# Heads 72 to 79 of a tree attention kernel stored by GpSimd in seventeen small DMAs instead of by GpSimd and SyncE in three

## The chip, the cores and the metric

The kernel runs on one core of a Trainium2 chip. The core has five instruction streams: TensorE (PE in the profile), VectorE (DVE), ScalarE (ACT), GpSimd (POOL) and SyncE (SP). Bytes between the device memory and the on-chip memory are moved by 16 DMA engines; DMAs are issued here from GpSimd (queue q0 of the profile), SyncE (q1) and ScalarE (q10). The metric is the device time in microseconds (us); lower is better.

## The reference

Q, K and V are float32 tensors of 8 batches, 12 heads, 512 positions and 64 dimensions. The positions are the nodes of a binary heap, and each node attends to itself and its ancestors:

```python
mask[i, i] = 1
parent = i
while parent > 0:
    parent = (parent - 1) // 2
    mask[i, parent] = 1

scores = np.einsum('bhqd,bhkd->bhqk', Q, K) * scale
scores = scores + (1 - mask) * (-1e9)
weights = np.exp(scores - np.max(scores, axis=-1, keepdims=True))
weights = weights / (np.sum(weights, axis=-1, keepdims=True) + 1e-10)
return np.einsum('bhqk,bhkd->bhqd', weights, V).astype(np.float32)
```

The output is as large as one input: 96 heads (batch and head together) of 128 KB each, 12.6 MB.

## The kernel before, in words

The 96 heads are worked through in 48 steps of two heads. A step makes the scores of its pair (`scores1`, `scores2`, with the mask put in by small matmuls of codes), takes exponentials on ScalarE, multiplies by V on TensorE (`values`, L551) and divides by the row sums on VectorE (`norm`, a reciprocal at L581 and a product at L583). Transposes of K and Q for later steps and copies of V rows (`spread`, L336) go between.

`norm` writes into a buffer `of` of eight heads (128 partitions, each with 8 heads x 4 positions x 64 numbers). There are twelve such groups and eleven buffers. A partition holds four neighbouring positions of a head, which are 1 KB in a row of the output. `store` (L590) writes some heads and some partitions of such a group to the output; every store has the line L591.

The order of work on each engine is written out by hand. GpSimd has one list of its own, made by `pool_program` (L606): loads of K, Q and V, which change float32 to bf16 on the way, copies of V rows, and stores of whole groups. `ready` (L648) says from which step on the next entry may be emitted, and entries are emitted in the list's order, so a GpSimd instruction that waits holds up everything behind it in the list. The last entries are stores: groups of eight heads up to head 71, then heads 72 to 75, then heads 80 to 87.

SyncE has the rest: at step 41 (`APART_AT`) `store_apart` (L601) stores heads 76 to 79 in two DMAs, of 60 and of 68 partitions, and the last four steps' heads (88 to 95) go out in three stores of two heads and one of one head, with the very last head on ScalarE (L768 to L771).

Waits between engines and on DMAs are put in by the framework when the program is compiled. A DMA that GpSimd issues gets one of eight semaphores in turn. In the compiled program each carries a wait for its semaphore's previous use, and so for the landing of the DMA eight places before it, beside any wait for data.

Of the kernel before, what the change touches and what calls it, by code (L numbers as in the profile page):

```python
# [119 lines left out]
def kernel(  # L120
# [7 lines left out]
    nc = tc.nc  # L128
    B, H, S, D = Q.shape
    P = nc.NUM_PARTITIONS  # L130
# [6 lines left out]
    KB, VB = 8, 16  # L137
# [307 lines left out]
    def turn(name, i):  # L445
        heads = [head(i + b, a) for b in range(2 if i >= WIDE else 1) for a in range(2)]
        assert all((name, h) in issued for h in heads), (name, i)
        {"kst": (narrow_k, wide_k), "qst": (narrow_q, wide_q)}[name][i >= WIDE](i)
        return i + (2 if i >= WIDE else 1)
# [4 lines left out]
    def scores1(i):  # L454

        sp = psS.tile([P, 2, 512], fp32, name="s1")
        for a in range(2):
            nc.tensor.matmul(  # L458
                out=sp[:, a, :],
                lhsT=(k1code if i < WIDE else k1wide)[64 * a:64 * a + CODE_ROWS, :],  # L460
                rhs=(q1code[64 * a:64 * a + CODE_ROWS, :] if i < WIDE
                     else q1wide[64 * a:64 * a + CODE_ROWS, :, :]),
                start=True, stop=False,
            )
        for a in range(2):
            nc.tensor.matmul(  # L466
                out=sp[:, a, :], lhsT=keys(i, a, TOP),
                rhs=qTs[i][64 * a:64 * a + 64, :, :].rearrange("p t c -> p (t c)"),
                start=False, stop=True,
            )  # L470
        et = etpool.tile([P, 2, 4, 128], bf16, name="e1")
        nc.scalar.activation(  # L472
            out=et[:, :, :, :].rearrange("p a t c -> p (a t c)"),
            in_=sp[:, :, :].rearrange("p a c -> p (a c)"),
            func=AF.Exp, scale=scale,
        ) if i < WIDE else nc.scalar.activation(  # L476
            out=et[:, :, :, :].rearrange("p a t (r u) -> p a (t r) u", u=2),
            in_=sp[:, :, :].rearrange("p a (u c) -> p a c u", u=2),
            func=AF.Exp, scale=scale,
        )  # L480
        ets[i] = et
# [92 lines left out]
    def norm(i):  # L574
        j, r = divmod(i, 4)
        if r == 0:
            ofs[j] = opool.tile([P, 8, 4, D], fp32, name="of")
        o4 = obs[i][:, :, 0:260].rearrange("p a (t c) -> p a t c", c=D + 1)
        rec = small.tile([P, 2, 4, 1], fp32, name="rec")
        for a, n in ((0, 2),) if i < NP - 1 else ((0, 1), (1, 1)):  # L580
            nc.vector.reciprocal(out=rec[:, a:a + n, :, :], in_=o4[:, a:a + n, :, D:D + 1])  # L581
            h0, h1 = [head(i, x) % 8 for x in (a, a + n - 1)]
            nc.vector.tensor_tensor(  # L583
                out=ofs[j][:, h0:h1 + 1:head(i, 1) - head(i, 0), :, :],
                in0=o4[:, a:a + n, :, 0:D],
                in1=rec[:, a:a + n, :, :].to_broadcast([P, n, 4, D]),
                op=ALU.mult,
            )

    def store(eng, h0, n, step=1, p0=0, p1=P):  # L590
        return eng.dma_start(  # L591
            out=Or[p0:p1, h0:h0 + step * (n - 1) + 1:step, :],
            in_=ofs[h0 // 8][p0:p1, h0 % 8:h0 % 8 + step * (n - 1) + 1:step, :, :].rearrange(
                "p h t d -> p h (t d)"
            ),
        )

    APART, APART_AT, APART_ROWS = 76, 41, 60

    def store_apart():  # L601

        for p0, p1 in ((0, APART_ROWS), (APART_ROWS, P)):
            store(nc.sync, APART, 4, 1, p0, p1)

    def pool_program():  # L606

        ops = [
            (load_k, 2, 2), (load_q, 2, 2), (load_v, 0, 4), (load_v, 4, 4),
            (load_k, 4, 2), (load_k, 6, 2), (load_q, 4, 2), (load_k, 8, 4),  # L610
            (load_q, 6, 2), (load_q, 8, 4), (load_v, 8, 8), (load_k, 12, 4),
            (load_q, 12, 4), (load_k, 16, 4), (load_rows, 1, "upper"),
            (load_q, 16, 4), (load_rows, 1, "even"), (load_k, 20, 4), (load_rows, 1, "odd"),
            (load_q, 20, 4), (load_k, 24, 8), (load_q, 24, 4), (load_rows, 2, "upper"),
            (load_q, 28, 4), (load_k, 32, 4), (load_rows, 2, "even", "odd"),
            (load_q, 32, 8), (load_k, 36, 4), (load_rows, 3, "upper"),
            (spread_pool, (1, "Z0", 8, 16), (1, "Z1", 8, 16), (1, 6, 8, 16), (1, 9, 8, 16)),
            (load_k, 40, 8), (load_q, 40, 8), (load_rows, 3, "even", "odd"), (spread_top, 2),
            (spread_pool, (2, "Z0", 0, 16), (2, "Z1", 0, 16), (2, "X", 0, 16)),
            (spread_top, 3, 0, 4), (load_q, 48, 4),  # L620
            (spread_top, 3, 4, 8), (load_k, 48, 8), (load_q, 52, 4), (spread_top, 3, 8, 12),
            (load_rows, 4, "upper"), (spread_top, 3, 12, 16),
        ]
        loaded, stored = 72, 0
        for h in range(56, NH, KB):
            top = [(spread_top, h // VB + 0)] if h % VB == 8 and 4 <= h // VB + 0 < NH // VB else []
            if top:
                top.append((spread_pool, (h // VB, "Z0", 0, 16), (h // VB, "Z1", 0, 16)))
            ops += [(load_k, h, KB)] + top + [(load_q, h, KB)]
            if h == 64:  # L630
                ops.append((spread_pool, (3, "Z0", 0, 16), (3, "Z1", 0, 16), (3, "X", 0, 16)))
            while loaded < min(h + 32, NH):
                names = ("even", "odd") if loaded % VB else ("upper",)
                ops.append((load_rows, loaded // VB) + names)
                loaded += KB
            if top:
                o = h // VB
                ops.append((spread_pool, (o, "X", 0, 16)))
            if stored + KB + BEHIND <= h + KB:
                ops.append((store, nc.gpsimd, stored, KB))  # L640
                stored += KB
        while stored < NH - KB:
            n = 4 if stored + 4 == APART else KB
            ops.append((store, nc.gpsimd, stored, n))
            stored += KB
        return ops

    def ready(op, i):  # L648

        f, args = op[0], op[1:]  # L650
        if f in (load_k, load_q):
            return 2 * (i + 3) >= args[0] + args[1] - 4 * KB
        if f is load_v:
            return True
        if f is load_rows:
            return 2 * i >= VB * (args[0] - 2)
        if f is spread_pool:
            return 2 * i >= VB * (args[0][0] + 1 - NV) and all(
                part != "X" or ("vt", "M", VB * o + h) in issued
                for o, part, h0, h1 in args for h in range(h0, h1)  # L660
            )
        if f is spread_top:
            return 2 * i >= VB * (args[0] + 1 - NV)
        return 2 * i >= args[1] + args[2]

    BY_VECTOR = {
# [69 lines left out]
    for i in range(NP + 1):  # L736
        steps = FIRST[i] if i < len(FIRST) else "SVK" if i % 2 else "SVQ"
        for step in steps:
            if step == "S" and i < NP:
                scores1(i)  # L740
                scores2(i)
            if step == "V" and i >= 1:
                values(i - 1)
                norm(i - 1)
                valued = True
            if step == "K" and kdone < NP:
                kdone = turn("kst", kdone)
            if step == "Q" and qdone < NP:
                qdone = turn("qst", qdone)
            if step == "W":  # L750
                nc.scalar.copy(
                    out=codes[64:64 + CODE_ROWS, 1280:1536], in_=codes[0:CODE_ROWS, 1280:1536]
                )
            if step == "X":
                spin("s1" if valued else "ob", 2)
            if step == "D":
                spread_by(nc.vector.tensor_copy, BY_VECTOR, STEADY_VECTOR, i)
            if step == "A":
                spread_by(nc.scalar.copy, BY_SCALAR, {}, i)
        if "D" not in steps:  # L760
            spread_by(nc.vector.tensor_copy, BY_VECTOR, STEADY_VECTOR, i)
        if "A" not in steps:
            spread_by(nc.scalar.copy, BY_SCALAR, {}, i)
        pool(i)
        if i == APART_AT:
            store_apart()
        if i >= NP - 3 and i < NP:
            store(nc.sync, head(i - 1, 0), 2, 2)  # L768
    assert not program
# [32 lines left out]
```

## Time and profile before

| | |
|---|---|
| time, median of 2 runs | 134.98 us (134.3 and 135.66) |
| the profiled execution's own time | 134.74 us |
| its span | 132.9 us |
| PE, DVE, ACT, POOL busy | 85%, 76%, 70%, 57% of the span |
| read from and written to device memory | 37.94 MB and 12.58 MB, 380 GB/s over the span |
| last exponential, last product of `norm` | before 125 us, at 126.3 us |
| stores issued by GpSimd | 11, the last at 119.1 us |
| stores issued by SyncE and ScalarE | 6 and 1, from 108.8 to 126.3 us |

The span is the time from the first to the last instruction in the trace; the device time has a little around it. Times in the trace count from the start of the span. In the page's line of 40 slices each digit is the busy share of a slice in tenths. In a timeline row come the start, the duration, the engine, the line, the operation, what it writes and reads, how many, and in brackets how long its engine was idle before it and what ended that. The landing of a DMA is the moment from which whoever waits for it may go on.

### The profile page before, as it was taken

How to read it: one execution, taken by the hardware profiler on the slowest of the kernel's cores; microseconds unless marked ns; L12 is line 12 of the kernel's file. 1: busy time of each engine (PE TensorE's matmuls, PEld its weight loads, DVE VectorE, ACT ScalarE, POOL GpSimd, SP SyncE). 2: the span in 40 equal slices, each digit the busy share in tenths (PEclk: the TensorE clock that was granted, in tenths of full speed). 3: DMA queues.
4: the chain of work that ended last, by engine and by line, in shares of the span. 5: the costliest groups of instructions: out<-in, count | busy, mean ns of one | idle time of the engine just before them, and what ended most of it. 6: DMA issues, size and time to landing. Idle time of an engine off the chain costs nothing.

```text
span 132.9 us, 5533 instructions
## 1 busy us (share of the span) xinstructions
PE 113.1 (85%) x2417; PEld 78.5 (59%) x2417; DVE 100.6 (76%) x249; ACT 93.6 (70%) x151; POOL 76.2 (57%) x112
## 2 busy tenths in 40 slices
PE   6785979999899899989989999996899998989600
PEld 2342765766566577656767575674576775665400
DVE  3439779887999989969797797887779986865600
ACT  4359678988587597858859687686598986869400
POOL 6989635265296979999596796569585400011000
PEclk9999999999999999999999999999999999999965
DMA  3999999999999999999999999999999999999981
GB/s 101 240 188 195 201 196 201 200 202 206 200 202 203 202 204 205 200 206 201 205 204 200 311 256 202 288 280 243 328 219 335 227 299 401 402 400 398 386 321 56
DMA packets 32221, 32.26 MB, mean 243 GB/s; under 512 B 1181, under 2 KB 29469, under 8 KB 32197
## 3 DMA queue, kind: packets, MB, share of 16 engines
q0 software_dynamic: 29824, 29.63, 114.2%
q1 hardware_dynamic: 1813, 1.83, 4.0%
q10 hardware_dynamic: 560, 0.46, 1.2%
q8 instruction: 19, 0.31, 0.9%
q14 instruction: 5, 0.04, 0.1%
HBM read 37.94 MB, written 12.58 MB: 380 GB/s over the span
## 4 chain that ended last, share of the span: by engine, by line
PE 41%; DMA 28%; DVE 11%; POOL 10%; issue 4%; ACT 1%; DVEq 0%; ACTq 0%; POOLq 0%
DMA vst<-in_V_dram 16%; PE ob L551 14%; DMA qst<-in_Q_dram 12%; PE s L458 7%; PE qtp L433 4%; PE ktp L401 4%; PE s L466 4%; PE s L501 4%; PE s L491 4%; POOL vt L336 3%; DVE vt L336 3%; DVE of L583 3%; POOL kst L239 2%; POOL qst L239 2%; POOL vst L239 1%
## 5 line engine op out<-in xcount | busy, mean ns | idle before, releaser
L476 ACT ACTIVATE e<-s 128x1024 bf16<-128x1024 f32 x40 | 41.0, 1024 | 22.0 <-PE s L466 22.0
L551 PE MATMUL ob<-vt,e 128*128 128x65 bf16 (+1 forms) x940 | 37.6, 197 | 3.3 <-DVE of L583 1.4
L551 PEld LDWEIGHTS <-e 128*128 128x128 bf16 (+1 forms) x960 | 30.4, 102 | 11.6 <-DVE of L583 1.5
L507 ACT ACTIVATE e<-s 128x384 bf16<-128x384 f32 x80 | 34.7, 490 | 0.0
L583 DVE TENSOR_TENSOR of<-ob,rec 128x512 f32<-128x512 f32 x47 | 32.5, 691 | 1.6
L336 POOL COPY vt<-vst 32x128 int32<-32x128 int32 (+3 forms) x44 | 27.4, 622 | 6.2 <-DVE vt L336 3.9
L336 DVE COPY vt<-vst 64x1024 bf16<-64x1024 bf16 (+6 forms) x42 | 18.4, 438 | 3.4 <-DMA vst<-in_V_dram 2.8
L458 PE MATMUL s<-codes 40*128 40x512 bf16 x96 | 19.5, 394 | 1.0 <-issue 0.4
L581 DVE RECIPROCAL rec<-ob 128x8 f32<-128x8 f32 x47 | 9.7, 205 | 13.4 <-PE ob L551 12.5
L591 POOL DMA_DIRECT2D out_dram<-of x11 | 9.8, 893 | 17.2 <-DVE of L583 12.7
L466 PE MATMUL s<-kq 64*128 64x512 bf16 x96 | 18.5, 377 | 0.0
L280 POOL DMA_DIRECT2D vst<-in_V_dram x15 | 11.1, 743 | 9.1 <-DMA vst<-in_V_dram 5.6
L501 PEld LDWEIGHTS <-kq 64*128 64x128 bf16 x320 | 12.4, 94 | 5.1 <-issue 0.5
L501 PE MATMUL s<-kq 64*128 64x160 bf16 (+1 forms) x320 | 14.9, 208 | 0.3 <-issue 0.3
L401 PE MATMUL ktp<-ptile,kst 128*64 128x128 bf16 x320 | 12.6, 220 | 2.1 <-DMA kst<-in_K_dram 1.0
L441 DVE COPY kq<-qtp 128x1024 bf16<-128x1024 bf16 x20 | 13.6, 682 | 0.7 <-PE qtp L433 0.7
L433 PE MATMUL qtp<-ptile,qst 128*64 128x128 bf16 x320 | 12.6, 220 | 1.8 <-issue 0.9
L491 PE MATMUL s<-codes 40*128 40x384 bf16 x80 | 13.8, 334 | 0.1
L251 POOL DMA_DIRECT2D qst<-in_Q_dram x13 | 9.5, 728 | 4.7 <-DMA qst<-in_Q_dram 1.7
L251 POOL DMA_DIRECT2D kst<-in_K_dram x12 | 9.2, 763 | 5.0 <-PE s L466 1.5
L401 PEld LDWEIGHTS <-kst 128*64 128x64 bf16 x320 | 9.9, 110 | 2.7 <-issue 1.3
L472 ACT ACTIVATE e<-s 128x1024 bf16<-128x1024 f32 x8 | 8.2, 1023 | 4.6 <-PE s L466 4.5
(42 smaller groups left out, 115.3 us busy)
## 6 DMA issues: line engine op xcount, KB each, us to landing
out_dram<-of POOLq DMA_DIRECT2D x10, 1024.0 KB, 17.3
kst<-in_K_dram POOLq DMA_DIRECT2D x8, 512.0 KB, 15.0
qst<-in_Q_dram POOLq DMA_DIRECT2D x7, 512.0 KB, 15.4
vst<-in_V_dram POOLq DMA_DIRECT2D x12, 256.0 KB, 12.7
vst<-in_V_dram POOLq DMA_DIRECT2D x6, 512.0 KB, 12.8
qst<-in_Q_dram POOLq DMA_DIRECT2D x8, 256.0 KB, 11.0
kst<-in_K_dram POOLq DMA_DIRECT2D x6, 256.0 KB, 11.7
out_dram<-of SPq DMA_DIRECT2D x3, 256.0 KB, 7.3
```

Of the source, the lines that this page charges most:

```text
L251: return nc.gpsimd.dma_start(out=kept[b][:, h0 % KB:h0 % KB + n, :, :].rearrange("p (g x) t d -> p g (x t d)", x=2), in_=wide[:, h0 // 2:( ...
L336: return copy(out=dst, in_=src)
L401: nc.tensor.transpose(out=columns(kp[64 * a:64 * a + 64, :], mixed, (256, 2), (leaves - mixed, 2), (1, 32)), in_=st[:, 2 * i % KB // 2 + a ...
L433: nc.tensor.transpose(out=halves[64 * a:64 * a + 64, :, c:c + 64], in_=st[:, 2 * i % KB // 2 + a, 4 * u + t, :], identity=ptile[:, 0:128],)
L458: nc.tensor.matmul(out=sp[:, a, :], lhsT=(k1code if i < WIDE else k1wide)[64 * a:64 * a + CODE_ROWS, :], rhs=(q1code[64 * a:64 * a + CODE_ ...
L466: nc.tensor.matmul(out=sp[:, a, :], lhsT=keys(i, a, TOP), rhs=qTs[i][64 * a:64 * a + 64, :, :].rearrange("p t c -> p (t c)"), start=False, ...
L476: ) if i < WIDE else nc.scalar.activation(
L491: nc.tensor.matmul(out=flat[:, a, :, :].rearrange("p u (t c) -> p u t c", t=4)[:, :, :, 16:64], lhsT=k2wide[64 * a:64 * a + CODE_ROWS, :], ...
L501: nc.tensor.matmul(out=flat[:, a, :, lo:hi], lhsT=keys(i, a, WTILE2[t]), rhs=qT[64 * a:64 * a + 64, :, lo:hi], start=False, stop=t == 1, s ...
L507: nc.scalar.activation(out=e2s[i % NE][:, a, :, 32:128].rearrange("p t (r u) -> p t r u", u=2), in_=flat[:, a, :, :].rearrange("p u (t r) ...
L551: nc.tensor.matmul(out=ob[lo:hi, a, 65 * t:65 * t + 65], lhsT=e[:, a, PLACE[t], lo:hi], rhs=vt[vtile[tile_v][0]][:, head(i, a) % VB, vtile ...
L583: nc.vector.tensor_tensor(out=ofs[j][:, h0:h1 + 1:head(i, 1) - head(i, 0), :, :], in0=o4[:, a:a + n, :, 0:D], in1=rec[:, a:a + n, :, :].to ...
```

## The change

GpSimd takes over heads 76 to 79 as well. Heads 72 to 75 become eight DMAs of 17, 17, 17, 17, 17, 17, 17 and 9 partitions, heads 76 to 79 become nine of 7, seven times 17, and 2 partitions. An instruction ahead of the first one sets the turn in which GpSimd's DMAs are dealt to DMA engines back to the first engine. The intent of the number 17 is that a DMA of 17 rows isn't divided among engines. `ready` lets each of the two groups go once its four heads are normalised. The two stores of SyncE go away; all other stores stay.

```diff
-    APART, APART_AT, APART_ROWS = 76, 41, 60
-
-    def store_apart():
-
-        for p0, p1 in ((0, APART_ROWS), (APART_ROWS, P)):
-            store(nc.sync, APART, 4, 1, p0, p1)
+    APART = {72: (17,) * 7 + (9,), 76: (7,) + (17,) * 7 + (2,)}
+
+    def store_apart(h0):
+
+        if h0 == 72:
+            nc.gpsimd.inc_swdge_sem([], [], mode="reset_dge_cursor")
+        p0 = 0
+        for n in APART[h0]:
+            store(nc.gpsimd, h0, 4, 1, p0, p0 + n)
+            p0 += n
+        assert p0 == P
...
         while stored < NH - KB:
-            n = 4 if stored + 4 == APART else KB
-            ops.append((store, nc.gpsimd, stored, n))
+            if stored in APART:
+                ops += [(store_apart, h) for h in APART]
+            else:
+                ops.append((store, nc.gpsimd, stored, KB))
             stored += KB
...
+        if f is store_apart:
+            return 2 * i >= args[0] + 4
...
         pool(i)
-        if i == APART_AT:
-            store_apart()
         if i >= NP - 3 and i < NP:
```

On GpSimd's list the cursor instruction and the 17 stores stand behind the store of heads 64 to 71 and ahead of the store of heads 80 to 87.

## The prediction

> **What bounds the kernel now.** I read the page's slices first, then busy time and DMA by stretches, then the timeline of GpSimd, then the DMA issues of short stretches. The page:
>
> ```profile
> span 132.9 us, 5533 instructions
> ...
> DMA  3999999999999999999999999999999999999981
> GB/s 101 240 188 195 201 196 201 200 202 206 200 202 203 202 204 205 200 206 201 205 204 200 311 256 202 288 280 243 328 219 335 227 299 401 402 400 398 386 321 56
> ...
> q0 software_dynamic: 29824, 29.63, 114.2%
> q1 hardware_dynamic: 1813, 1.83, 4.0%
> ```
>
> The DMA engines are busy from the second slice to the last but one. q0 is GpSimd's queue, q1 is SyncE's. After the last loads the stores move some 400 GB/s. The stretches, in columns PE, PEld, DVE, ACT, POOL, granted clock, DMA share, GB/s:
>
> ```profile
> 109.00:112.00 3.00, 2.34 (x58) 1.58 (x51) 2.02 (x6) 1.82 (x4) 0.00 (x0) 1.00 1.03 398
> 112.00:116.00 4.00, 4.00 (x101) 2.92 (x96) 2.78 (x7) 3.44 (x6) 0.00 (x0) 1.00 1.03 397
> 116.00:120.00 4.00, 3.31 (x80) 2.48 (x77) 2.46 (x7) 2.84 (x5) 0.88 (x1) 1.00 1.03 404
> 120.00:124.00 4.00, 3.83 (x70) 2.36 (x70) 1.77 (x4) 3.82 (x8) 0.01 (x1) 1.00 1.02 395
> 124.00:126.00 2.00, 1.06 (x21) 0.74 (x20) 1.73 (x6) 0.49 (x2) 0.00 (x0) 1.00 0.99 382
> 126.00:128.00 2.00, 0.00 (x0) 0.00 (x0) 0.29 (x1) 0.00 (x0) 0.00 (x0) 0.84 0.99 367
> 128.00:130.00 2.00, 0.00 (x0) 0.00 (x0) 0.00 (x0) 0.00 (x0) 0.00 (x0) 0.50 0.71 240
> 130.00:133.00 3.00, 0.00 (x0) 0.00 (x0) 0.00 (x0) 0.00 (x0) 0.00 (x0) 0.50 0.12 41
> ```
>
> Compute is over at about 126.3 and the stores then drain, so the end is a matter of stores. At 397 GB/s a store of 1 MB (8 heads) costs 2.64 us on all engines, and one engine moves 397/16 = 24.8 GB/s. The drain is ragged: what is left after 128 is 2 x 0.71 + 3 x 0.12 = 1.8 us of all 16 engines, yet it takes 3.1 us; the unevenness is worth 1.3 us.
>
> Now GpSimd, which issues all stores but the last few (start, duration, idle before and who ended it):
>
> ```profile
> 70.06 0.66 POOL L280 DMA_DIRECT2D vst<-in_V_dram  x1
> 71.14 0.65 POOL L280 DMA_DIRECT2D vst<-in_V_dram  x1 [0.41 <-DMA qst<-in_Q_dram]
> 72.45 0.90 POOL L591 DMA_DIRECT2D out_dram<-of  x1 [0.67 <-DMA vst<-in_V_dram]
> 74.04 0.76 POOL L251 DMA_DIRECT2D kst<-in_K_dram  x1 [0.69 <-PE s L466]
> ...
> 79.59 0.74 POOL L251 DMA_DIRECT2D qst<-in_Q_dram  x1
> ...
> 82.54 0.91 POOL L591 DMA_DIRECT2D out_dram<-of  x1
> 83.44 0.76 POOL L251 DMA_DIRECT2D kst<-in_K_dram  x1
> 85.16 0.74 POOL L251 DMA_DIRECT2D qst<-in_Q_dram  x1 [0.96 <-DMA qst<-in_Q_dram]
> 86.30 0.91 POOL L591 DMA_DIRECT2D out_dram<-of  x1 [0.40 <-DMA vst<-in_V_dram]
> ...
> 97.81 3.56 POOL L591 DMA_DIRECT2D out_dram<-of  x4
> 103.02 0.89 POOL L591 DMA_DIRECT2D out_dram<-of  x1 [1.66 <-DVE kq L412]
> 105.67 0.76 POOL L591 DMA_DIRECT2D out_dram<-of  x1 [1.76 <-DVE vt L336]
> 119.12 0.90 POOL L591 DMA_DIRECT2D out_dram<-of  x1 [12.69 <-DVE of L583]
> ```
>
> The row at 86.30 is the important one. It is a store, which reads `of` and writes the output, and what let it go is the landing of a load of V. No data joins the two. The DMA issued at 70.06 is the eighth before it, and it landed 15.9 us after its issue (row below), at 86.0. GpSimd's DMAs take eight completion semaphores in turn, and each waits until the one eight before it has landed. In this trace the limit costs GpSimd a few tenths of a us at a time, since what it issues is large.
>
> The landings that the sum needs (us from issue to landing, each DMA alone in its stretch of the DMA view; the fourth row is the store at 119.12):
>
> ```profile
> vst<-in_V_dram POOLq DMA_DIRECT2D x1, 256.0 KB, 15.9
> ...
> out_dram<-of POOLq DMA_DIRECT2D x1, 1024.0 KB, 14.9
> ...
> out_dram<-of POOLq DMA_DIRECT2D x1, 1024.0 KB, 21.2
> ...
> out_dram<-of POOLq DMA_DIRECT2D x1, 1024.0 KB, 9.8
> ...
> out_dram<-of ACTq DMA_DIRECT2D x1, 128.0 KB, 5.3
> ```
>
> The store at 97.81 landed at 112.7, the one at 103.02 (heads 64 to 71) at 124.2, the one at 119.12 (heads 80 to 87) at 128.9, and ScalarE's, issued at 126.3, at 131.6, the last of all. The span ends 1.3 later at 132.9.
>
> **The change, part by part.** *Removed*: one 512 KB store of heads 72 to 75 on GpSimd, and on SyncE the two stores of heads 76 to 79 (60 and 68 rows). *Added on GpSimd*: the cursor instruction and 17 small stores (eight for 72 to 75, nine for 76 to 79), all ahead of the store of heads 80 to 87. Loads and compute keep their place: GpSimd's last load is issued at 94.0, before any of this, and behind the small stores only that one store is queued. Bytes are the same.
>
> *The cursor instruction* has no row. It stands in idle time (1.76 us before the row at 105.67), so between 0 and that it costs nothing; that it waits for the queue to empty is a rival.
>
> *Eight semaphores.* In the compiled program each of the 17, and the store of heads 80 to 87, waits for its semaphore. Numbering the small ones 1 to 17 and the last store 18: numbers 2 and 3 wait for loads, 4 to 8 for the five 1 MB stores issued from 97.81 to 103.02, number 9 for number 1, 10 for 2, 17 for 9, and **18 for number 10**. Today the last store waits at 119.12 for VectorE alone.
>
> Step 1, number 8's gate: heads 64 to 71 must have landed on all engines, 124.2 today. The first of the five landed at 112.7, so without SyncE's stores between them it is 112.7 + 4 x 2.64 = 123.3. Check: from 112 on, SyncE's queue moved 0.24 + 0.09 + 0.10 MB,
>
> ```profile
> q1 hardware_dynamic: 240, 0.24, 16.9%
> ...
> q1 hardware_dynamic: 98, 0.09, 6.8%
> ...
> q1 hardware_dynamic: 102, 0.10, 7.3%
> ```
>
> (stretches 112 to 116, 116 to 120, 120 to 124), 1.1 us at 397 GB/s, which gives 124.2 - 1.1 = 123.1. Bounds: 122.0 (no unevenness, 123.3 - 1.3) and 124.2.
>
> Step 2, number 1 lands. Its 17 rows of 4 KB go to one engine: 69,632 bytes at 24.8 GB/s are 2.8 us, behind that engine's share of the five stores. If the engine runs ahead of the slowest by 2.8 us it adds nothing, if it is the slowest it adds 2.8. No row tells which engine is slow, so I take the middle: 123.3 + 1.4 = 124.7 (bounds 122.0 and 127.0). Number 2 is then as far on the next engine.
>
> Step 3, number 9 goes at 124.7 and number 10 one issue later. An issue of 512 rows took 0.66 us (70.06), one of 1024 rows 0.89; the line through them gives 0.46 for 17 x 4 rows. I take 0.5 (bounds 0.36, the shortest of SyncE's below, and 0.66): 125.2.
>
> ```profile
> L591 SPq DMA_DIRECT2D out_dram<-of x6: 357/390/793, 108.8 to 125.8; - x6
> ...
> kst<-in_K_dram POOLq DMA_DIRECT2D x1, 128.0 KB, 4.5
> ...
> ptile<-tree_eye ACTq DMA_DIRECT2D x1, 64.0 KB, 2.6
> ```
>
> Step 4, number 10 lands. Now its queue is dry, so the start and finish of a DMA, hidden so far by what was queued, show. GpSimd's first load (4.5 us to landing for 128 KB, 0.3 us of transfer) gives 4.2 at most. It shared the engines with 256 + 256 + 120 + 64 KB of other first loads, 1.8 us, which leaves 2.4; the 64 KB load of ScalarE on idle engines also gives 2.6 - 0.2 = 2.4. I take 2.5, with bounds 2.4 and 4.2. Number 10 lands at 125.2 + 2.5 + 2.8 = 130.5. The nine issues from number 9 on would let 18 go at 124.7 + 4.5 = 129.2, so the landing decides: **the last store goes at 130.5 instead of 119.1**.
>
> Step 5, it lands: 130.5 + 2.5 + 2.64 = 135.6. Number 16, issued at 128.2, holds its engine until 133.5 by the same terms, 0.5 longer than the last store would leave it waiting: 136.1. SyncE's and ScalarE's last stores are issued by 126.3 and meet half-empty engines; they land before that.
>
> The Trainium skill, page "DMA: Bandwidth & Descriptors", section on the anatomy of a GpSimd DMA, fits a DMA at 2.0 us plus its bytes at 436 GB/s; by it the last store would take 4.4 us where I have 5.1, and the time would be 0.7 lower. Row and rule can't be told apart on this trace, where GpSimd's later DMAs are always queued.
>
> Sum: landing 136.1, end of span 1.3 later at 137.4, and the profiled execution's own time lies 134.74 - 132.9 = 1.84 above its span: **139.2 us**. The profiled execution of before is 0.24 under the median of the two runs (134.98), so I leave it at 139.2, 3.1% slower.
>
> **The rivals.** *Spread after all (13%).* The small stores go to several engines, two rows each. Number 1 then adds 2 x 4 KB, 0.33 us, instead of 2.8, and number 10 no longer takes 2.8 us. Only issues count: number 8 at 123.3, ten issues of 0.5 to the last store at 128.3, landing 133.4, time 133.4 + 1.3 + 1.84 = 136.6. Against it: 17 rows don't divide; for it: every GpSimd store in this trace was spread. The Trainium skill (same page, section "Why a DMA increments its semaphore by 16 and not by 1") says that the engine count is the largest number up to 16 that divides the rows, so one for 17, but notes an exception on trn2 in which GpSimd's direct copies are spread all the same, by the rows over 16 rounded up. No GpSimd DMA of before has a row count by which the two differ.
>
> *Not slower: the relief decides (6%).* 272 KB of SyncE's stores were drained at a crawl (some 25 packets a us after 116, rows above), ahead of SyncE's last stores. Without them the drain evens out and gains up to 1.3 us: 134.74 - 1.3 = 133.4. It decides only if the last store goes early enough to land by 131.6, so at 131.6 - 5.1 = 126.5 or sooner. That needs numbers 9 to 17 not to hold it, against the row at 86.30.
>
> *One engine for all (3%).* The turn doesn't move on, and all 17 go to the same engine: 1 MB at 24.8 GB/s is 42 us behind 122, the last store's share behind that, some 170 us.
>
> *The cursor waits for the queue (8%).* Number 1 then goes only at 123.3 and lands at 123.3 + 0.5 + 5.3 = 129.1, number 10 at 129.1 + 0.5 + 5.3 = 134.9, the last store at 140.5: 143.7.
>
> **How the numbers follow.** My forecast has 70%. Its own range: all low bounds give 122.0 + 0.36 + 5.2 + 5.0 = 132.6, time 135.7; all high ones 127.0 + 0.66 + 7.0 + 7.3 = 142.0, time 145.1, which needs every term at its worst, so I keep 135.7 to 143.0 for it. With the spread case below (136.6, about 1 us either way) and the waiting cursor at the top, the range is 135.5 to 143.2. About 2% is what a measurement of this kernel can tell from no change, that is up to 137.7 on one side and down to 132.3 on the other. A fifth of my forecast lies under 137.7. Slower: 0.56 of my forecast, 0.03 of the spread case, 0.11 of the last two: 0.70. Faster: a third of the relief, 0.02. Within 2%: 0.28.
>
> **What would show it.** Step 1: numbers 4 to 8 on GpSimd 2.6 us apart, each ended by the landing of a store. Steps 2 to 4: number 9 near 125, the store of heads 80 to 87 near 130, its wait ended by a DMA and no longer by VectorE; landing of a small one after a dry queue near 5.3. Step 5: a DMA share well under 1 from about 124 to 131, with engines idle while stores remain, and then one burst of 1 MB at the end. PE, VectorE and ScalarE unchanged until 126. I am wrong if the last store goes before 127, if the small ones are issued without waits, or if their landings show that engine 0's turn is long past.

## The result, and the profile after

The changed kernel takes 149.44 us (149.06 and 149.81) against 134.98 before: a ratio of 1.1075, with an interval of 1.1007 to 1.1142. (An execution that took over 1.5% longer than the fastest of the same kernel is left out of the times and ratios in this document.) The direction was forecast; the size was not. 139.2 was predicted, in a range that ended at 143.2. So the question for the experiments is what cost 10 us more than the waits that the prediction counted.

The page of the changed kernel, span, slices, packet sizes and GpSimd's queue, and behind it the packet sizes of the kernel before:

```profile
span 146.2 us, 5547 instructions
...
DMA  3999999999999999999999999999999999885371
GB/s 126 211 184 195 198 199 201 201 206 202 201 203 201 204 206 200 204 201 207 199 306 247 202 323 233 314 243 298 260 284 398 402 385 176 119 211 124 57 258 50
DMA packets 35673, 32.31 MB, mean 221 GB/s; under 512 B 5018, under 2 KB 32794, under 8 KB 35650
...
q0 software_dynamic: 33808, 30.21, 108.7%
...
DMA packets 32221, 32.26 MB, mean 243 GB/s; under 512 B 1181, under 2 KB 29469, under 8 KB 32197
```

Up to slice 33 it is the kernel before. In the next two slices the engines still show busy (9 and 8 in the DMA line) while the rate falls from some 400 to 176 and 119 GB/s. The packets tell of what: 5018 are under 512 bytes, where the kernel before has 1181. In the trace 3600 of them are packets of 16 bytes on GpSimd's queue, and the kernel before has none of that size. The stretches of the changed kernel, in the columns of the prediction:

```profile
116.00:120.00 4.00, 3.37 (x78) 2.31 (x72) 2.98 (x8) 2.58 (x6) 1.09 (x2) 1.00 1.01 392
120.00:124.00 4.00, 3.77 (x76) 2.40 (x70) 2.17 (x5) 3.82 (x7) 1.98 (x2) 1.00 1.01 203
124.00:126.00 2.00, 1.23 (x30) 0.86 (x26) 0.18 (x1) 1.45 (x3) 0.75 (x2) 1.00 0.83 72
126.00:128.00 2.00, 0.73 (x17) 0.52 (x14) 1.84 (x6) 0.00 (x0) 1.66 (x3) 0.87 0.93 167
128.00:130.00 2.00, 0.00 (x0) 0.00 (x0) 0.00 (x0) 0.00 (x0) 1.77 (x2) 0.50 0.96 219
130.00:134.00 4.00, 0.00 (x0) 0.00 (x0) 0.00 (x0) 0.00 (x0) 2.32 (x4) 0.50 0.70 166
134.00:138.00 4.00, 0.00 (x0) 0.00 (x0) 0.00 (x0) 0.00 (x0) 3.52 (x4) 0.50 0.35 65
138.00:142.00 4.00, 0.00 (x0) 0.00 (x0) 0.00 (x0) 0.00 (x0) 0.00 (x0) 0.50 0.71 220
```

From 120 to 124 the share is 1.01 at 203 GB/s, half the rate of before, and from 124 to 126 it is 0.83 at 72. That isn't the picture of engines that wait, which the prediction expected. GpSimd's timeline:

```profile
106.16 1.11 POOL L591 DMA_DIRECT2D out_dram<-of  x1 [1.93 <-DVE vt L336]
108.17 1.08 POOL L591 DMA_DIRECT2D out_dram<-of  x1 [0.90 <-DMA kst<-in_K_dram]
111.06 1.06 POOL L591 DMA_DIRECT2D out_dram<-of  x1 [1.81 <-DMA qst<-in_Q_dram]
113.34 1.06 POOL L591 DMA_DIRECT2D out_dram<-of  x1 [1.22 <-DMA out_dram<-of]
115.91 1.06 POOL L591 DMA_DIRECT2D out_dram<-of  x1 [1.51 <-DMA out_dram<-of]
119.87 1.06 POOL L591 DMA_DIRECT2D out_dram<-of  x1 [2.91 <-DMA out_dram<-of]
122.44 1.06 POOL L591 DMA_DIRECT2D out_dram<-of  x1 [1.52 <-DMA out_dram<-of]
125.06 0.58 POOL L591 DMA_DIRECT2D out_dram<-of  x1 [1.56 <-DMA out_dram<-of]
125.84 0.56 POOL L591 DMA_DIRECT2D out_dram<-of  x1 [0.20 <-issue]
126.73 2.14 POOL L591 DMA_DIRECT2D out_dram<-of  x2 [0.34 <-DMA out_dram<-of]
129.10 2.10 POOL L591 DMA_DIRECT2D out_dram<-of  x2 [0.23 <-issue]
131.95 1.07 POOL L591 DMA_DIRECT2D out_dram<-of  x1 [0.75 <-DMA out_dram<-of]
133.95 3.57 POOL L591 DMA_DIRECT2D out_dram<-of  x4 [0.93 <-DMA out_dram<-of]
```

The eight semaphores are there as forecast: numbers 2 and 3 wait for loads, 4 to 8 for large stores, and the waits end by DMAs. But a store of 17 partitions takes 1.06 to 1.11 us to issue, against 0.56 to 0.58 for 9, 7 or 2 partitions, and longer than one of 1024 rows (0.89). Number 8 goes at 125.06, number 9 at 125.84, number 10 at 126.73, and the store of heads 80 to 87 at the end of the last row, at 136.59 instead of 119.1. Issue to landing, of number 1, number 10 and that last store, each from a short stretch of the DMA view:

```profile
out_dram<-of POOLq DMA_DIRECT2D x1, 68.0 KB, 19.1
...
out_dram<-of POOLq DMA_DIRECT2D x1, 68.0 KB, 8.9
...
out_dram<-of POOLq DMA_DIRECT2D x1, 1024.0 KB, 8.2
```

Number 1 landed at 125.2, number 10 at 135.7, the last store at 144.8, and the span ends 1.4 later. Of the chain that ended last (start, duration, what), this is the part ahead of the last store:

```profile
122.44 11.22 DMA out_dram<-of
133.67 0.28 issue
133.95 1.76 POOL out_dram L591 x2
```

The DMA issued at 122.44 is number 7, and what waited for its landing at 133.67 is number 15.

### The profile page after: what moved, and what is told of

Read it like the earlier page. It is cut to its first block, busy times and chain, and to the rows that moved or that the text cites. A ratio compares the mean times of both kernels' runs of the same rounds, so it can differ in the third digit from the quotient of the medians.

```text
span 146.2 us, 5547 instructions
## 1 busy us (share of the span) xinstructions
PE 112.8 (77%) x2417; PEld 78.2 (54%) x2417; DVE 100.7 (69%) x249; ACT 93.6 (64%) x151; POOL 91.7 (63%) x128
## 2 busy tenths in 40 slices
DMA packets 35673, 32.31 MB, mean 221 GB/s; under 512 B 5018, under 2 KB 32794, under 8 KB 35650
## 4 chain that ended last, share of the span: by engine, by line
DMA 43%; PE 25%; DVE 11%; POOL 9%; issue 4%; ACT 1%; POOLq 1%; ACTq 0%
DMA out_dram<-of 22%; DMA qst<-in_Q_dram 10%; PE ob L551 8%; DMA kst<-in_K_dram 7%; DMA vst<-in_V_dram 5%; POOL vt L336 4%; PE s L458 4%; POOL out_dram L591 3%; DVE vt L336 3%; DVE of L583 3%; PE ktp L401 3%; PE qtp L433 2%; PE s L466 2%; PE s L501 2%; PE s L491 2%
## 5 line engine op out<-in xcount | busy, mean ns | idle before, releaser
L591 POOL DMA_DIRECT2D out_dram<-of x27 | 25.6, 949 | 18.5 <-DMA out_dram<-of 10.7
L280 POOL DMA_DIRECT2D vst<-in_V_dram x15 | 10.9, 726 | 8.3 <-DMA vst<-in_V_dram 5.5
## 6 DMA issues: line engine op xcount, KB each, us to landing
qst<-in_Q_dram POOLq DMA_DIRECT2D x7, 512.0 KB, 14.4
qst<-in_Q_dram POOLq DMA_DIRECT2D x8, 256.0 KB, 10.9
```

Of the source, the lines that this page charges most:

```text
L591: return eng.dma_start(out=Or[p0:p1, h0:h0 + step * (n - 1) + 1:step, :], in_=ofs[h0 // 8][p0:p1, h0 % 8:h0 % 8 + step * (n - 1) + 1:step, ...
```

## The experiments

Ten kernels were run. Where nothing else is said, the edit shown is of the changed kernel; four of the ten leave out the attention and only store zeros. Theory A says that a store of 17 partitions isn't only the affair of the engine that gets its data; theory W says that the chain of eight semaphores is the loss.

**One small store alone.** A kernel of stores of zeros by GpSimd:

```diff
+ALONE = (17, 17, 17, 9, 7, 2, 16, 15, 18, 32, 33, 128)
+BURSTS = ((17,) * 7, (16,) * 7)
...
+    for n in ALONE:
+        store(h0, 0, n)
+        settle()
+        h0 += 4
```

> Only stores, all of them by GpSimd, of zeros: heads 0 to 47 each get one store of 4 heads and n partitions, each issued after the one before has landed, n = 17, 17, 17, 9, 7, 2, 16, 15, 18, 32, 33, 128; then seven stores of 17 partitions in a row without a wait between them for data, and seven of 16. Theory A (filler): a 17-row store puts its data on one engine and sends packets of 16 bytes, about 17 of them, to each of the other 15, so in the packet counts a 17-row store shows 17 packets of 4 KB and about 255 of 16 bytes, its issue takes 1.06 us against about 0.57 for 2, 7, 9 and 16 rows, and seven in a row take about 1.1 us each (7 to 8 us until the last has landed, beyond the first); seven of 16 rows have no such packets and take the issue, 0.5 to 0.6 us each. Theory W (waits): the 16-byte packets cost next to nothing, a lone 17-row store lands after 2.5 + 2.8 = 5.3 us, a lone 16-row one after 2.5 + 0.2 = 2.7, and seven of 17 in a row on seven engines land within 5.3 us plus six issues.

The DMA view of the stretches with the second store of 17, the one of 16 and the one of 18:

```profile
DMA packets 288, 0.07 MB, mean 11 GB/s; under 512 B 271, under 2 KB 271, under 8 KB 288
...
out_dram<-of POOLq DMA_DIRECT2D x1, 68.0 KB, 5.7
...
DMA packets 32, 0.07 MB, mean 19 GB/s; under 512 B 16, under 2 KB 16, under 8 KB 32
...
out_dram<-of POOLq DMA_DIRECT2D x1, 64.0 KB, 2.2
...
DMA packets 48, 0.07 MB, mean 21 GB/s; under 512 B 30, under 2 KB 30, under 8 KB 48
...
out_dram<-of POOLq DMA_DIRECT2D x1, 72.0 KB, 2.3
```

Each store has 16 completion packets of 4 bytes. Beside those, 16 partitions are 16 packets of 4 KB and nothing else. 18 partitions are 18 packets of 4 KB and 14 small ones. 17 partitions are 17 packets of 4 KB and 255 small ones of 16 bytes, 15 times 17. A GpSimd DMA has sixteen marks of its landing in the trace, one for each engine. Of this store one comes at 5.7, the other fifteen at 2.8 to 3.1. The trace doesn't name the engine of a packet, but counts and landings fit this reading: the data went to one engine, as the prediction had it, and each of the others was sent one small packet for each row. In the changed kernel fourteen stores of 17 make 14 x 255 = 3570 of the 3600, and those of 9, 7 and 2 partitions showed 7, 9 and 14 here, the other 30. The issue took 1.06 to 1.21 us for 17 and 0.53 to 0.59 for 2, 7, 9, 15, 16 and 18. The seven stores of 17 in a row took from 58.74 to 73.17, 14.4 us, and the seven of 16 from 74.9 to 80.2, 5.3. Theory W's price for a lone one (5.3) is nearly right; its price for seven in a row (5.3 and six issues of 1.06, 11.7) is short by 2.8. Theory A's for the six behind the first (7 to 8 us) is short by 0.4.

**16 partitions instead of 17.**

```diff
-    APART = {72: (17,) * 7 + (9,), 76: (7,) + (17,) * 7 + (2,)}
+    APART = {72: (16,) * 8, 76: (16,) * 8}
```

> As the changed kernel, but heads 72 to 79 go out in sixteen stores of 16 partitions instead of seventeen of mostly 17: the same queue, the same waits on eight semaphores (one fewer), the same bytes. Theory A (filler): no 16-byte packets, each store costs its engines 0.17 us, what is left is the wait for number 1 (about 123.5) and nine issues of 0.57: the store of heads 80 to 87 goes at about 129 and lands at 134 to 135, time 137 to 139 us. Theory W (waits): what makes the changed kernel 14 us slower is the chain of eight semaphores, which is the same here: time 146 to 150.

138.17 us, 1.024 of before (1.0201 to 1.0279): within theory A's numbers, 8 us off theory W's. GpSimd's timeline:

```profile
121.32 0.51 POOL L591 DMA_DIRECT2D out_dram<-of  x1 [2.09 <-DMA out_dram<-of]
124.17 5.46 POOL L591 DMA_DIRECT2D out_dram<-of  x10 [2.34 <-DMA out_dram<-of]
```

Number 8 waits for the large store as in the changed kernel. From there all goes without another wait, at 0.51 each. The last store is issued at 128.72 and lands at 133.7. So small stores in GpSimd's queue, their chain of semaphores and their issues together, cost 3.2 us (138.17 against 134.99 for one store, below), and the shape of 17 the other 11. Not all of the 3.2 is waiting: of the 2.8 us between the two profiled spans (135.9 and 133.1), 1.5 lie before the last landing (133.7 against 132.1) and 1.3 behind it, where the end comes 2.2 us after that landing instead of 1.0. There GpSimd's closing instruction, a drain, ends only at 135.1; why it takes longer wasn't tried.

**18 partitions.**

```diff
-    APART = {72: (17,) * 7 + (9,), 76: (7,) + (17,) * 7 + (2,)}
+    APART = {72: (18,) * 7 + (2,), 76: (18,) * 7 + (2,)}
```

> As the changed kernel with 18 partitions in place of 17 (seven of 18 and one of 2 for each of the two groups of heads; sixteen stores). Alone, a store of 18 partitions showed 18 packets of 4 KB and only 14 of 16 bytes, was issued in 0.59 us and landed in 2.3 us on all engines. Theory A (filler): it is the shape of 17 that costs, so the time falls back to that of sixteen partitions: 137.5 to 140 us. Theory B (any small store that doesn't divide evenly over 16 engines costs the same): 146 to 150.

138.56 us, 1.0241 (1.0167 to 1.0315), the time of 16. One partition more per store, and the 11 us are gone. That a store doesn't divide evenly over sixteen engines is not the cause by itself.

**No cursor instruction.**

```diff
-        if h0 == 72:
-            nc.gpsimd.inc_swdge_sem([], [], mode="reset_dge_cursor")
```

> As the changed kernel without the cursor instruction. If that instruction costs time or makes GpSimd wait, 2 us or more less than 149.4; if it doesn't (both theories above), 149.4 within 1 us: it only decides which engine gets which 17 rows, and each engine gets as many in the end.

149.4 us (148.64 and 150.16), 1.1063 (1.0996 to 1.1131), against 1.1075: it costs nothing that can be measured, and the rival in which it waits for the queue is out. That it does no good either shows only that the first engine of the turn doesn't matter here.

**Heads 72 to 79 as one store by GpSimd.** An edit of the kernel before.

```diff
-            n = 4 if stored + 4 == APART else KB
+            n = KB
...
-        if i == APART_AT:
-            store_apart()
```

> The kernel before with heads 72 to 79 as one store of eight heads by GpSimd like the groups ahead of it; neither SyncE's two stores nor small ones. By the relief that the prediction priced at up to 1.3 us: 133.4 to 134.5 us. If SyncE's two stores cost nothing because the engines were full anyway: 135.0, as before. Should GpSimd's queue end later with more in it: 135.5 to 136.

134.99 us, 0.9994 (0.9972 to 1.0016), as expected for engines that were full anyway. The relief that the prediction priced at up to 1.3 us doesn't show: without SyncE's two stores GpSimd's queue holds the same bytes, and the drain is as ragged (DMA share 0.64 from 128 to 130 and 0.11 from 130 to 133, where it was 0.71 and 0.12). The last landing of this kernel is at 132.1, on SyncE's queue, against 131.6 before.

**Half the dose.** Heads 72 to 75 in stores of 17 by GpSimd, heads 76 to 79 by SyncE as before.

```diff
-    APART = {72: (17,) * 7 + (9,), 76: (7,) + (17,) * 7 + (2,)}
+    APART = {72: (17,) * 7 + (9,)}
...
+        if i == 41:
+            for p0, p1 in ((0, 60), (60, P)):
+                store(nc.sync, 76, 4, 1, p0, p1)
```

> Half the dose: heads 72 to 75 by GpSimd in stores of 17, 17, 17, 17, 17, 17, 17 and 9 as changed, heads 76 to 79 by SyncE in two stores as before. The store of heads 80 to 87 then waits for number 1 alone. Theory A (filler): number 1 lands near 125.2 as in the changed kernel and the last store goes at 125.7, but seven stores' filler (about 1.1 us on every engine each) lies ahead of it in the queue, so it lands near 134 to 136: time 138 to 141. Theory W (it is only the wait for the eighth before): issue 125.7 and 5.1 to landing: 134 to 135.

142.15 us, 1.0523 (1.0442 to 1.0604), half of the loss for half of the stores. That is above theory A's range by 1 us and 7 us above theory W's. The last store here waits for number 1 alone:

```profile
125.19 0.58 POOL L591 DMA_DIRECT2D out_dram<-of  x1 [1.55 <-DMA out_dram<-of]
128.32 0.93 POOL L591 DMA_DIRECT2D out_dram<-of  x1 [2.55 <-DMA out_dram<-of]
```

It was issued at 128.32 instead of the expected 125.7, since number 1 landed only at 127.8 (125.2 in the changed kernel). Both theories missed that. SyncE's store of 68 partitions, which this kernel has and the changed one hasn't, has marks of its landing at 125.5, 126.2, 128.1 and 129.2; that number 1 stood beside it on one of its engines would fit, but isn't shown. The last store then took 9.8 us to land, where a store of 1 MB behind sixteen stores of 16 partitions took 4.9. These are the rows of the half dose and of the kernel with 16:

```profile
out_dram<-of POOLq DMA_DIRECT2D x1, 1024.0 KB, 9.8
...
out_dram<-of POOLq DMA_DIRECT2D x1, 1024.0 KB, 4.9
```

**The last store by SyncE.** The changed kernel, with heads 80 to 87 out of the chain.

```diff
-            else:
+            elif stored < 80:
                 ops.append((store, nc.gpsimd, stored, KB))
...
+        if i == 44:
+            store(nc.sync, 80, KB)
```

> The changed kernel with the store of heads 80 to 87 issued by SyncE, which waits for VectorE alone, as soon as its heads are done (about 119). Takes the last store's 17 us of waiting behind the small ones away and leaves the seventeen stores. Theory A (filler and issue): the small ones go at the same pace and number 17 is still issued at about 136 and lands at 140 to 142: 143 to 146 us. Theory W (the wait of the last store is the loss): the small ones end by 132: 135 to 138 us.

146.22 us (146.21 to 147.87), 1.0846 (1.0747 to 1.0946), at the upper end of theory A's range; theory W had 135 to 138. The large store was issued at 118.27 and landed at 130.5. The seventeen went on as before, the last one issued at 137.10 and landed at 142.9. The 17 us by which the prediction's key store was late were thus worth about 3 us of time. The small stores alone hold the end at 146.

**Beside another queue.** Four stores of 512 KB by SyncE, alone, beside seven of 17 by GpSimd, beside seven of 16, and alone again.

```diff
+BURSTS = ((), (17,) * 7, (16,) * 7, ())
...
+        for k in range(4):
+            store(nc.sync, h0 + 4 + 4 * k, 4, 0, P)
```

> Only stores of zeros, in four stages: four stores of 512 KB by SyncE alone; the same beside seven GpSimd stores of 17 partitions; the same beside seven of 16; alone again. Tells whether the 16-byte packets hold up other queues, or only GpSimd, which takes 1.06 us to issue such a store. Alone the four should land within 8 us. If the filler holds the engines (a packet of 11 ns in the trace takes its engine some 60 ns), the store of SyncE is late on all engines beside the stores of 17, by 2 us or more at half of the sixteen landings, and by under 1 us beside those of 16. If it only takes GpSimd's time, half of the engines land as alone.

From SyncE's first issue to the landings of its fourth store: alone 7.4 to 7.6 us on all sixteen engines, in both stages. Beside 17, the first engine landed at 9.5, half of them by 10.0 and the last at 15.5. Beside 16, 9.4, 10.0 and 10.9. The store of SyncE is late on every engine beside 17, by 1.8 us at least, though in that stage seven stores put data on at most seven engines. That fits small packets that take other queues' time. But beside 16 it is late by as much at half of the engines, where under 1 us was expected. There each engine had seven packets of 4 KB to take, 1.2 us, so part of that lateness has another source, and the same may be so beside 17. This run doesn't separate the two theories at the middle, only at the late end.

**Issue time hidden.** GpSimd's queue is filled with four large stores first.

```diff
+BURSTS = ((17,) * 4, (16,) * 4, (18,) * 4)
...
+        for k in range(4):
+            store(h0, 7, 0, P)
+            h0 += 7
```

> Only stores of zeros by GpSimd, three stages, each of four stores of 7 heads (128 partitions, 0.9 MB) and behind them four small ones of 4 heads, of 17 partitions in the first stage, 16 in the second, 18 in the third. All eight are issued before the engines have done the four large ones, so the issue time is hidden and the steps from landing to landing of the small ones are what they cost the engines. Theory A1 (the 16-byte packets hold the engines): at half of the sixteen engines a store of 17 takes 0.4 to 1.1 us, a store of 16 or 18 some 0.2 to 0.3 us. Theory A2 (only GpSimd's 1.06 us of issue counts): at half of the engines 17 takes no more than 16 and 18, under 0.3 us.

All eight DMAs of the first stage were issued by 11.2 us and the fourth large store landed at 15.8 to 17.9, so no issue was awaited:

```profile
3.04 8.20 POOL L29 DMA_DIRECT2D out_dram<-of  x8 [2.60 <-DVE of L26]
26.19 5.80 POOL L29 DMA_DIRECT2D out_dram<-of  x8 [14.95 <-DVE of L44]
43.69 6.11 POOL L29 DMA_DIRECT2D out_dram<-of  x8 [11.70 <-DVE of L44]
```

From the landing of the last large store to that of the fourth small one, at the middle of the sixteen engines, four stores of 17 took 3.9 us, four of 16 took 1.6 and four of 18 took 1.7: 1.0 us a store against 0.4 (0.2 to 0.3 was expected for 16 and 18). At the first engine to land it was 3.4, 1.5 and 1.3; four stores of 17 put data on at most four engines, so the first to land is one of the twelve or more without. At the last engine it was 5.9, 0.8 and 1.1. So the small packets hold engines even when GpSimd's issue is long done: theory A1.

**Other row counts.**

```diff
+ALONE = (19, 31, 20, 34, 37, 48, 51, 60, 64, 68, 96, 100, 113, 127)
```

> Only stores of zeros by GpSimd of 4 heads and n partitions, each alone: n = 19, 31, 20, 34, 37, 48, 51, 60, 64, 68, 96, 100, 113, 127. Which row counts behave like 17. If data go to one engine where no number of rows per engine from n/16 (rounded up) divides n but n itself: 19, 31, 37, 113 and 127 show n packets of 4 KB and 15 n of 16 bytes and land late (n x 0.165 us on one engine), the others don't. If it is by n/16 rounded up alone, 17 was an exception and all land in 2.2 to 3.5 us.

The packets of 16 bytes by partitions: 285 for 19, 465 for 31, 555 for 37, 1695 for 113 and 1905 for 127, each 15 times the rows; 238 for 34, 221 for 51, 204 for 68, 60 for 100, 12 for 20, 4 for 60, none for 48, 64 and 96. These, and the counts of the first run, all follow if a store uses the largest number of engines up to 16 that divides its rows, and each engine left out gets one packet for each row that a used engine has: 34 is two engines of 17 rows, 14 x 17 = 238. The expectation had the primes right and missed that 34, 51 and 68 suffer too. They took 1.06 to 1.11 us to issue and landed in 5.9 to 6.9, where 64 took 2.9. The worst case, 127 partitions, against 100:

```profile
DMA packets 2048, 0.55 MB, mean 17 GB/s; under 512 B 1921, under 2 KB 1921, under 8 KB 2048
...
out_dram<-of POOLq DMA_DIRECT2D x1, 508.0 KB, 31.0
...
DMA packets 176, 0.41 MB, mean 59 GB/s; under 512 B 76, under 2 KB 76, under 8 KB 176
...
out_dram<-of POOLq DMA_DIRECT2D x1, 400.0 KB, 5.0
```

The Trainium skill, page "DMA: Bandwidth & Descriptors", section "Why a DMA increments its semaphore by 16 and not by 1", gives the rule of the largest divisor, which all 24 row counts tried here fit. Its exception on trn2 for some copies by GpSimd, rows spread by a sixteenth rounded up with 100 on fifteen engines and 127 on sixteen, was seen in none: the counts for 100 and 127 are those of ten engines and of one. The expectation's price for a late landing, 0.165 us a row, was too low: 127 rows would be 21 us, and their packets ran for 25 of the 31.0, 0.2 us a row.

## Why the prediction was wrong

*The drain and the small edits.* The drain bounds the end, as said. Compute ended 1.7 us later (ScalarE's store behind the last product was issued at 128.0 instead of 126.3). The stores that wait for it landed by 136.0, so it doesn't set the end. The cursor instruction costs nothing (149.4 without it).

*The eight semaphores* were right as a mechanism: GpSimd's waits are for the eighth DMA before, as the prediction had them. Sixteen stores of 16 partitions cost 3.2 us (138.17 against 134.99 with one store). That this is near the 4.2 forecast for the whole change is luck, since the forecast's chain has 1.4 and 2.8 us of data on one engine, which those stores don't have. It is the sum of the spread case that fits them: the last store at 128.3 and its landing at 133.4, and 128.72 and 133.7 were measured.

*Step 1* missed by more than its bounds: number 8's gate opened at 124.8, against 123.3 and bounds of 122.0 to 124.2. The 0.9 us taken off the 124.2 of before for SyncE's stores aren't there: without them and without small stores the gate opened at 124.3 (one store by GpSimd). That number 1 landed at 125.2, near the forecast 124.7, is two errors that cancel, a gate 1.5 us later and a landing 0.4 behind it instead of 1.4.

*Step 2 failed in its last sentence*, by which number 2 is then as far on the next engine. Numbers 2 to 8 landed at 126.5, 127.2, 128.5, 129.7, 131.7, 133.7 and 133.8, one after the other and not side by side.

*Step 3 failed in its price.* The issue was put on a line through the issues of 512 and 1024 rows, 0.46 for 68 rows, and taken as 0.5, with 0.66 as the upper bound. It took 1.06 for 17 partitions, and the nine issues from number 9 on took 8.6 us instead of 4.5. Rows of data were the wrong measure, since 17 partitions on one engine cost GpSimd more than 128 on sixteen (0.78).

*Step 4 failed.* Number 10 landed 8.9 us after its issue, against 5.3. The prediction took its queue to be dry. In fact every engine had to work through the small packets of the stores ahead, 1.0 us a store instead of the 0.4 of a store of 16 (hidden-issue run). Nor did this landing let the last store go, as step 4 has it. It came at 135.7, and GpSimd was still issuing: number 15 had waited for number 7 until 133.67, and its issue and two more came before the last store.

*Step 5 failed for the same reason.* The last store took 8.2 us instead of 5.6.

The sum of the misses: the last store was issued at 136.59 instead of 130.5, 6.1 (number 9 went 1.1 later than forecast; from it to the last store 5.8 were forecast, the issues alone took 2.8 more than that, and waits for landings another 2.2); its landing 2.6; the end of the span 0.1; the time outside the span 149.06 - 146.2 = 2.9 instead of 1.84, 1.0. Together 9.8 of the 9.9 us between 139.2 and the profiled execution's 149.06. The last 1.0 outside the span need not come from the change: in executions of the kernel before, that rest is between 1.7 (134.54, span 132.8) and 3.1 (135.74, span 132.6).

One assumption stands behind the end of step 2 and behind steps 4 and 5: that a DMA "to one engine" leaves the other fifteen free. The trace of before could not show the opposite, as no GpSimd DMA in it has a row count that leaves engines out, and it has no packet of 16 bytes. How much of the 11 us is small packets, how much issue and how much the data's 17 rows on one engine wasn't separated in the kernel itself: no kernel had such data without the small packets.

*The order of causes was wrong too.* The prediction let the late last store decide. Taken out of the chain it gave back about 3 of the 14.5 us. The sum followed one DMA's wait and never counted what seventeen of them cost the engines.

*The rivals.* Spread after all: not so, the data went to one engine. Not slower by relief: the relief isn't there (0.9994). One engine for all: not so, since seven in a row on one engine are 7 x 2.8 = 19.6 us of data alone, and they took 14.4 with everything. The waiting cursor: not so. The bounds left out what was unknown about the operation itself. With the longest issue of a store in the trace of before, 0.98 us, as the upper end for an unseen shape, nine issues would have put the last store at 124.7 + 8.8 = 133.5, still 3 us early. The engines taken for free were the larger error: 2.2 us of waits and 2.6 of landing, against the 2.8 of issues.

## What to carry to other kernels

Choose the partitions of a GpSimd DMA so that a number close to 16 divides them: multiples of 16 had no filler (those packets of 16 bytes), 15, 18, 20 and 60 had 1 to 14 packets of it, and 17, 19, 31, 34, 51, 68 and 127 had 204 to 1905. Of the last seven only 17 was tried in the attention kernel. When a trace shows engines busy at a falling rate, read the packet sizes before looking for waits. Where DMAs take a fixed number of completion semaphores in turn, many small ones put the next large one behind them: sixteen without filler cost 3.2 us here.

## What the runs showed that was not expected

A GpSimd DMA that leaves engines out sends each of them one packet of 16 bytes for every row of a used engine; this is read from counts and landings, and all 24 row counts fit it. In the trace such a packet lasts 11 ns at the median, so the busy share understates it: four stores of 17, 68 such packets on an engine, took 3.4 us on the engine that landed first, 50 ns each if they took all of it. The lone stores give much the same without a queue: the first engine landed 1.7 us after the end of the issue with 17 partitions, 2.5 with 31, 6.9 with 113 and 7.6 with 127, some 53 ns for each row more. Why a packet holds its engine over four times as long as the trace shows was not tried.

The issue time of GpSimd follows the rows of one used engine: 0.5 to 0.6 us up to two rows, 0.85 at ten (100 partitions), 1.06 at 17 and 4.55 at 127, near a line of 0.52 us and 0.032 for each row.
